# The gate matrix in DRAM by groups of four expert rows

## The chip, the cores and the metric

The kernel runs on one core of one Trainium2 chip. The metric is the device time in microseconds (us) of one execution. Five engines work beside each other: TensorE (PE, with its weight loads PEld), VectorE (DVE), ScalarE (ACT), GpSimd (POOL) and SyncE (SP). Each takes its instructions in a fixed order. Sixteen DMA engines move data between DRAM and the on-chip memory. In this trace q1 is the queue of the transfers that SyncE issues, q10 that of ScalarE's, and q0 that of GpSimd's.

## What is computed

The reference is a block of two layers over 256 latent and 256 context tokens of width 1024. Each layer has a mixer and then PEER, a feed-forward part that chooses among 16384 experts. Only PEER matters here:

```
s      = query . keys                      # 8 heads, 2 halves of 128 keys
idx    = the 16 best pairs (i1, i2) of each head, expert = 128 * i1 + i2
gate   = softmax(their scores)
act    = gelu(x . expert_u[idx])
out    = sum of gate * act * expert_v[idx]
```

Each token so uses 128 of the 16384 experts.

## The kernel before, in words

**Dense over all experts.** For most tokens the kernel doesn't gather: it multiplies every token with every expert and uses a gate that is zero for experts that were not chosen. The experts lie as 128 rows (i1, called `e` in the code) of 128 (i2). For each `e`, `U(e)` multiplies the tokens with the 128 `expert_u` rows of that `e` and applies gelu; `V(e)` multiplies the result with the gates, elementwise, and then with the 128 `expert_v` rows, and adds to the output that stays in PSUM. The experts lie on the partitions, the tokens on the free axis. Layer 0 does so for 384 tokens (three blocks of 128), layer 1 for 192 (a block and a half). The tokens left over (128 in layer 0, 64 in layer 1) are done by gathering rows with GpSimd (`gather_rows`, L1289), their sums on VectorE.

**The gate matrix.** Its entry for i2 = partition p, i1 = e and token t is the gate of expert (e, p) for t, or zero. `gates` (L1195) builds it with one-hot matrices: VectorE compares the chosen indices with a ramp, TensorE multiplies the one-hots of i2 and of i1 for each token, and ScalarE copies the result from PSUM into a tile `gst` of `[128, 128, 32]` (p, e, t) for a group of 32 tokens. There are 12 groups in layer 0 and 6 in layer 1. A full tile (2 MB) is sent to DRAM from ScalarE's queue (L1263), and its first few rows (`HOLD`, 4 in layer 0, 8 in layer 1) are copied to `gt0` on chip. `gst` has two buffers, so a tile can be filled again when the write of the group before the last one has landed.

**The order around it.** While the gates are built, the first U's run already (40 in layer 0, 64 in layer 1). Their results don't all fit: 22 in layer 0 and 32 in layer 1 go out to DRAM through the two buffers of `aout`, from ScalarE's queue too (L1403), and come back as `ain` through SyncE's queue (L1408), asked for two V's ahead, in three buffers. After the gates V starts, at first alone, and then U and V alternate. For every fourth `e`, V asks for the gates of four rows and all groups, through SyncE's queue, in which the weight loads `eraw` (L1356, five buffers), the spilled activations and, in layer 0, eight small loads of scores (L1276) stand as well:

```
gt[0] = p2.tile([128, ng, 4, 32], F32, name="gt", bufs=2)
nc.sync.dma_start(gt[0].rearrange("p g a b -> p g (a b)"),
                  gd.rearrange("g p x -> p g x")[:, :, 32 * e:32 * e + 128])
```

The multiply with the gates is L1423, the split of its result for the matmuls L1426 and L1427, the matmuls of V are L1445, those of U L78 in layer 0 and L1376 and L1380 in layer 1. Casts of weights into a high part are L72 (ScalarE), the low parts L73 (VectorE). `side()` puts the gathers between them.

**What sets the order.** The program is written as one stream, and a planner puts each engine's instructions in order by a modelled timeline, in which every instruction and DMA has a duration of the model. Waits are added by the framework: a DMA that reads a DRAM tile waits for the DMAs that wrote it. So a read of `gd` waits for all its writes.

Of the kernel before, what the change touches and what calls it, by code (L numbers as in the profile page):

```python
# [10 lines left out]
F32 = mybir.dt.float32  # L11
# [19 lines left out]
NI1 = 128  # L31
# [19 lines left out]
class Kernel:  # L51
# [1143 lines left out]
    def gates(self, l, blocks, es, ps):  # L1195

        nc = self.nc
        groups = [(b, tg) for b in blocks for tg in range(2 if b == self.half[l] else 4)]
        gd = self.dp.tile([len(groups), 128, NI1 * 32], F32, name=f"gd{l}", bufs=1)
        sels = {}  # L1200
        with self.pool(f"selx{l}", side="right") as sp:
            exps = {b: self.pick_exp(b, sp, len(blocks)) for b in blocks}
            for b in blocks:
                w = self.pick(b, sp, exps[b])
                if b == self.half[l]:

                    t = sp.tile([128, 128], F32, name="gixf", bufs=1)
# [15 lines left out]
                g = sp.tile([128, 2, 128], F32, name="gsel", bufs=2)  # L1223
# [9 lines left out]
        with self.pool(f"gate{l}", side="right") as p:  # L1233
            for gi, (b, tg) in enumerate(groups):
                sel = sels[b]
                if True:
                    st = p.tile([128, NI1, 32], F32, name="gst", bufs=2)
                    for q in range(32 // OHT):
                        t = 32 * tg + OHT * q
                        ts = (128, OHT, 64, 2)  # L1240
                        io = self.iota.rearrange("p (a b) -> p a b", b=2)[:, None].to_broadcast(ts)
                        at = lambda z: sel[:, z, t:t + OHT][:, :, None].to_broadcast(ts)
                        one = lambda nm: p.tile([128, OHT, 64, 2], F16, name=nm, bufs=OHB)
                        o2, o2s, oh, ol = one("oh2"), one("oh2s"), one("oh1h"), one("oh1l")
                        nc.vector.tensor_tensor(o2, io, at(1), op=OP.is_equal)
                        e = OSC[q % len(OSC)]
                        if e == "a":
                            nc.scalar.mul(o2s, o2, 2.0 ** -12)
                        else:
                            nc.vector.tensor_scalar(o2s, o2, 2.0 ** -12, None, op0=OP.mult)  # L1250
                        nc.vector.tensor_tensor(ol, io, at(0), op=OP.is_equal)
                        nc.vector.tensor_tensor(oh, ol, at(2), op=OP.mult)
                        nc.vector.tensor_tensor(ol, ol, at(3), op=OP.mult)
                        flat = lambda a, z: a[:, z].rearrange("p a b -> p (a b)")
                        for z0 in range(0, OHT, 4):
                            pb = ps.tile([128, 4, 128], F32, name="gps", tag="gps", bufs=GPS)
                            for z in range(4):
                                nc.tensor.matmul(pb[:, z, :], flat(o2, z0 + z), flat(oh, z0 + z), start=True, stop=False)
                                nc.tensor.matmul(pb[:, z, :], flat(o2s, z0 + z), flat(ol, z0 + z), start=False, stop=True)
                            o = OHT * q + z0  # L1260
                            nc.scalar.mul(st[:, :, o:o + 4], pb.rearrange("p t i -> p i t"), 2.0 ** -14)
                    nc.gpsimd.tensor_copy(self.gt0[:, gi], st[:, 0:HOLD[l], :])
                    nc.scalar.dma_start(gd[gi], st.rearrange("p i t -> p (i t)"))  # L1263
        return gd

    def gather_gen(self, l, b, es):
# [61 lines left out]
    def peer(self, l, dense):  # L1328
        nc, i = self.nc, self.i
# [7 lines left out]
        with ExitStack() as es:  # L1337
            p = es.enter_context(self.pool(f"peer{l}"))
# [8 lines left out]
            with self.pool(f"psg{l}", space=PSUM) as gp:  # L1347
                gd = self.gates(l, dense, es, gp)
# [3 lines left out]
            acts, gt, rows, todo, left, los = {}, {}, {}, [], [], []  # L1352

            def stream(src, nm):
                raw = p.tile([128, 1024], F32, name="eraw", bufs=ERAW)
                nc.sync.dma_start(raw, src)  # L1356
                hi = p.tile([128, 1024], F32R, name=nm + "hi", bufs=2)
                lo = p.tile([128, 1024], F32R, name=nm + "lo", bufs=2)
                self.split(hi, lo, raw)
                return hi, lo  # L1360
# [49 lines left out]
            def V(e):  # L1410
                if e < HOLD[l]:
                    gt[0] = self.gt0[:, :, e - e % 4:e - e % 4 + 4]
                elif e % 4 == 0:
                    gt[0] = p2.tile([128, ng, 4, 32], F32, name="gt", bufs=2)
                    nc.sync.dma_start(gt[0].rearrange("p g a b -> p g (a b)"),
                                      gd.rearrange("g p x -> p g x")[:, :, 32 * e:32 * e + 128])
                late = NI1 - 1 - e
                hi, lo = stream(i["v"][l, e], "u" if late < TOGETHER[l] and late % 2 else "v")
                a = acts.pop(e)
                av = a.rearrange("p (g t) -> p g t", t=32)  # L1420

                with self.after(*los[max(e - 2, 0):max(e - 1, 0)]):
                    nc.vector.tensor_tensor(av, av, gt[0][:, :, e % 4, :], op=OP.mult)  # L1423

                w = p2.tile([128, 2 * nt + nt % 128], F32R, name="whl", bufs=max(3, TOGETHER[l]))
                nc.scalar.copy(w[:, 0:nt], a)  # L1426
                self.v_lo = nc.vector.tensor_tensor(w[:, nt:2 * nt], a, w[:, 0:nt].bitcast(F32), op=OP.subtract)  # L1427
                if half is not None:
                    nc.scalar.copy(w[:, 2 * nt:], a[:, nt - nt % 128:])
                los.append(self.v_lo)  # L1430
                todo.append((e, hi, lo, w))
                if 0 < late < TOGETHER[l]:
                    return

                for b in range(nb) if half is None else (1, 0):
                    for hs in ((0,), (1,)) if late == 0 else ((0, 1),):
                        for e_, hi, lo, w in todo:
                            if 128 * b + 128 > nt:

                                ops = [(w[:, 2 * nt - 64:], r) for r in (hi, lo)]  # L1440
                            else:
                                ops = [(w[:, o:o + 128], r) for o, r in ((128 * b, hi), (128 * b, lo), (nt + 128 * b, hi))]
                            for z, (a_, r) in enumerate(ops):
                                for h in hs:
                                    nc.tensor.matmul(acc[b][h], a_, r[:, 512 * h:512 * h + 512],  # L1445
                                                     start=e_ == 0 and z == 0, stop=e_ == NI1 - 1 and z == len(ops) - 1)
                todo.clear()
# [10 lines left out]
            def pubank(shape, nm):  # L1458
                t = pu_.tile([128, 512], F32, name="pu", bufs=8 - 2 * nb)
                n = math.prod(shape[1:])  # L1460
                return t[:, :n] if len(shape) == 2 else t[:, :n].rearrange("p (a b) -> p a b", b=shape[2])
# [19 lines left out]
            for e in range(NI1):  # L1481
                if e == lead - KEEP:
                    es_b.close()
                    if not last:
                        sw = self.s5_ahead(l + 1, es_b.enter_context(self.pool(f"s5w{l + 1}")), pubank)
                back(e + AHEAD)
                if e + KEEP == NI1:
                    for _ in sw:
                        left.append(e)
                    es_b.close()  # L1490
                    ep = es.enter_context(self.pool(f"peere{l}", side="right"))
                    gr = {ty: self.mod_row(l, 5, ty, ep, 1, pubank, f"gaterow{ty}") for ty in sorted({b // 2 for b in dense})}
                V(e)
                if e >= KEEP - 1:
                    side()
                if e + KEEP >= lead and e + KEEP < NI1:
                    U(e + KEEP)
                    side()
                    if e % 4 == 3:
                        next(mg, None)  # L1500
                    if e % 3 == 2:
                        next(sw, None)
# [7 lines left out]
            if half is not None:  # L1510
# [4 lines left out]
                for h in range(2):  # L1515
                    t = ep.tile([128, 512], F32, name="ft", bufs=2)
                    nc.scalar.copy(t, acc[nb - 1][h])
                    b = pubank([128, 512], "fold")
# [4 lines left out]
            for k, b in enumerate(sorted(out) if half is None else (3, 2)):  # L1523
                ty = b // 2
                x = self.xk[b] = self.row([128, 1024], f"xe{b}")
                nc.sync.dma_start(x, self.xd[b])
                st = ep.tile([128, 2], F32, name="fst", bufs=2) if last else self.xst[:, b]
                for h in range(2):
                    hs = slice(512 * h, 512 * h + 512)
                    t = ep.tile([128, 512], F32, name="et", bufs=3)  # L1530
# [14 lines left out]
                else:  # L1545
                    nc.vector.tensor_tensor(st[:, 0:1], st[:, 0:1], st[:, 1:2], op=OP.add)
                    self.rstd(st[:, 1:2], st[:, 0:1], 1024)
                    if k == 0:
                        fg = ep.tile([128, 1024], F32, name="fg", bufs=1)
                        f = i["final_g"]  # L1550
# [126 lines left out]
```

## Time and profile before

| | us |
|---|---|
| median of 3 runs | 2690.12 (2687.3 to 2694.61) |
| the profiled execution | 2692.46 |
| its span, from the first instruction to the last | 2689.2 |
| PE busy | 2525.4 |
| DVE busy | 2185.1 |
| ACT busy | 1217.7 |

The mean granted TensorE clock is 0.972 of full speed. The DMA engines move 694.55 MB, at a mean of 258 GB/s. A share of busy time over the whole span mixes stages with different limits, so the stages are read one by one. The gate matrix is built and written from 540 to 700 us in layer 0 and from 2015 to 2110 in layer 1; V and U with its reads follow, to about 1600 and 2650. In the rows below a line number is that of the kernel before, and "x" a count. PE's busy time is that of pipelined matmuls, whose ends are modelled. The DMA share is the time that packets took, over 16 engines and the stretch; packets that run past the end of a stretch or wait within their time can lift it over 100%.

### The profile page before, as it was taken

What the parts mean: (1) busy time and instruction counts of PE and PEld (TensorE: products, weight loads), DVE (VectorE), ACT (ScalarE), POOL (GpSimd) and SP (SyncE); (2) the same over time, 40 slices, a digit from 0 to 9 for tenths busy, and PEclk for the clock granted to TensorE, in tenths of its full rate; (3) what the DMA queues carried; (4) which work ended last, traced back from release to release, by engine and by line L of the source; (5) the groups of instructions that cost most, each with busy time, mean ns of one, the idle gap of its engine ahead of it and who ended that gap; (6) DMA issues with size and microseconds to landing.
All of it is one profiled execution on the core that took longest, in us unless ns stands there. A gap on an engine that the chain in (4) does not pass through costs nothing.

```text
span 2689.2 us, 42483 instructions
## 1 busy us (share of the span) xinstructions
PE 2525.4 (94%) x15591; PEld 2141.6 (80%) x15591; DVE 2185.1 (81%) x4639; ACT 1217.7 (45%) x2054; POOL 593.8 (22%) x468
## 2 busy tenths in 40 slices
PE   7999999999999999999999999999888977999997
PEld 4776888888778898998899996878877855677786
DVE  8765489999888988998988855837989788999985
ACT  3343343566434333333333333444457644555564
POOL 0001000010004433444443400010001043444500
PEclk8998999999999999999999999989899999999999
DMA  7521432587779899999999956625477899999984
GB/s 271 135 94 41 156 109 93 179 296 280 261 242 371 302 342 333 340 342 331 329 340 335 337 184 176 227 96 192 160 247 264 286 338 331 384 381 381 384 299 141
DMA packets 269200, 694.55 MB, mean 258 GB/s; under 512 B 28608, under 2 KB 120576, under 8 KB 266432
## 3 DMA queue, kind: packets, MB, share of 16 engines
q1 hardware_dynamic: 192960, 430.57, 47.3%
q0 software_dynamic: 55296, 201.35, 20.6%
q10 hardware_dynamic: 20736, 59.92, 6.3%
q8 instruction: 122, 2.00, 0.3%
q14 instruction: 86, 0.70, 0.1%
HBM read 631.84 MB, written 58.56 MB: 257 GB/s over the span
## 4 chain that ended last, share of the span: by engine, by line
PE 41%; issue 12%; DVE 10%; DMA 6%; ACT 4%; ACTq 0%; POOL 0%; SPq 0%; DVEq 0%; POOLq 0%
PE acc L1445 20%; PE pu L78 14%; PE pu L1376 2%; DMA act<-aout 2%; DVE ulo L73 2%; DVE vlo L73 2%; PE pu L1380 1%; ACT uhi L72 1%; DVE grow L1306 1%; DMA ain<-act 1%; ACT vhi L72 1%; PE prT L286 1%; DVE wlo L73 1%; DMA raw<-in_w_in_dram 1%; DVE gacc L1313 1%
## 5 line engine op out<-in xcount | busy, mean ns | idle before, releaser
L1445 PE MATMUL acc<-vhi,whl 128*128 128x512 f32 x2274 | 662.3, 401 | 27.1 <-ACT whl L1426 19.6
L1445 PEld LDWEIGHTS acc<-vhi,whl 128*128 128x128 f32 x2274 | 428.1, 190 | 131.3 <-ACT whl L1426 26.7
L72 ACT CAST vhi<-eraw 128x1024 fp32r<-128x1024 f32 x253 | 265.0, 1048 | 344.1 <-PE acc L1445 308.1
L1445 PE MATMUL acc<-vlo,whl 128*128 128x512 f32 x1264 | 395.4, 404 | 14.5 <-DVE vlo L73 14.0
L78 PE MATMUL pu<-hTb,uhi 128*128 128x384 f32 x2048 | 390.9, 341 | 7.7 <-ACT uhi L72 3.8
L73 DVE TENSOR_TENSOR vlo<-eraw,vhi 128x1024 fp32r<-128x1024 f32 x253 | 309.0, 1223 | 106.9 <-ACT vhi L72 106.3
L1300 POOL DMA_INDIRECT grow<-in_un_dram,gidx x192 | 243.9, 1270 | 603.3 <-DVE grow L1306 198.6
L78 PEld LDWEIGHTS pu<-hTb,uhi 128*128 128x128 f32 x2048 | 362.2, 190 | 17.3 <-ACT actr L1396 4.7
L73 DVE TENSOR_TENSOR ulo<-eraw,uhi 128x1024 fp32r<-128x1024 f32 x259 | 316.7, 1223 | 72.3 <-ACT uhi L72 57.9
L72 ACT CAST uhi<-eraw 128x1024 fp32r<-128x1024 f32 x259 | 272.0, 1051 | 183.5 <-PE pu L78 171.8
L1300 POOL DMA_INDIRECT grow<-in_v_dram,gidx x192 | 271.2, 1412 | 347.1 <-DVE gacc L1313 215.9
L1376 PE MATMUL pu<-hTb,uhi 128*128 128x384 f32 x1024 | 320.7, 369 | 18.0 <-ACT uhi L72 16.0
L1445 PEld LDWEIGHTS acc<-vlo,whl 128*128 128x128 f32 x1264 | 238.9, 191 | 82.8 <-DVE vlo L73 28.7
L1380 PE MATMUL pu<-hTb,ulo 128*128 128x192 f32 x1024 | 250.2, 265 | 25.7 <-DVE ulo L73 24.8
L1313 DVE SCALAR_TENSOR_TENSOR gacc<-grow,gact,gacc 128x1024 f32<-128x1024 f32 x190 | 243.9, 1284 | 1.8 <-DMA grow<-in_v_dram,gidx 1.7
L286 PE MATMUL prT<-hTb,whi 128*128 128x512 f32 (+1 forms) x928 | 240.2, 346 | 3.5 <-ACT whi L72 3.2
L1306 DVE SCALAR_TENSOR_TENSOR grow<-grow,h2n 128x1024 f32<-128x1024 f32 x192 | 234.4, 1221 | 8.8 <-DMA grow<-in_un_dram,gidx 8.8
L1380 PEld LDWEIGHTS pu<-hTb,ulo 128*128 128x128 f32 x1024 | 198.6, 196 | 48.5 <-DVE ulo L73 41.4
L1376 PEld LDWEIGHTS pu<-hTb,uhi 128*128 128x128 f32 x1024 | 195.1, 193 | 27.6 <-ACT uhi L72 22.6
L78 PE MATMUL pu<-hTb,ulo 128*128 128x384 f32 x1024 | 204.0, 337 | 0.5 <-DVE ulo L73 0.5
L73 DVE TENSOR_TENSOR wlo<-raw,whi 128x1024 fp32r<-128x1024 f32 x84 | 102.4, 1220 | 114.0 <-ACT whi L72 111.3
L286 PEld LDWEIGHTS prT<-hTb,whi 128*128 128x128 f32 x928 | 159.8, 190 | 31.3 <-ACT whi L72 3.4
(435 smaller groups left out, 3839.6 us busy)
## 6 DMA issues: line engine op xcount, KB each, us to landing
eraw<-in_ut_dram SPq DMA_DIRECT2D x256, 512.0 KB, 5.6
eraw<-in_v_dram SPq DMA_DIRECT2D x256, 512.0 KB, 6.0
gd<-gst ACTq DMA_DIRECT2D x18, 2048.0 KB, 8.2
mraw<-in_w_mod_dram SPq DMA_DIRECT2D x64, 512.0 KB, 5.1
gt<-gd SPq DMA_DIRECT2D x31, 768.0 KB, 10.2
raw<-in_w_in_dram SPq DMA_DIRECT2D x36, 512.0 KB, 5.3
raw<-in_w_query_dram SPq DMA_DIRECT2D x32, 512.0 KB, 3.9
eraw<-in_w_mod_dram SPq DMA_DIRECT2D x32, 512.0 KB, 6.3
```

Of the source, the lines that this page charges most:

```text
L72: (hi_eng or nc.scalar.copy)(hi, src)
L73: self.last_lo = (lo_eng or nc.vector).tensor_tensor(lo, src, hi.bitcast(F32), op=OP.subtract)
L78: self.nc.tensor.matmul(out, a, b, start=n == 0, stop=n == len(ops) - 1)
L286: self.nc.tensor.matmul(bs[g][:, pt * n:pt * n + n], a[:, k, gs], b, start=z == 0 and k == 0 and q == 0, stop=z == 1 and k == 3 and q == 2)
L1300: nc.gpsimd.indirect_dma_start(out=r, out_offset=None, in_=src, in_offset=bass.IndirectOffsetOnAxis(ap=idx[:, j:j + 1], axis=0))
L1306: v.scalar_tensor_tensor(r, r, 1.0, self.h2n, op0=OP.mult, op1=OP.mult, accum_out=act[:, j:j + 1])
L1313: v.scalar_tensor_tensor(acc, r, act[:, j:j + 1], acc, op0=OP.mult, op1=OP.add)
L1376: both = lambda: nc.tensor.matmul(pu, hi[:, cs], self.hTb[:, :, c, c0:c0 + nt], start=c == 0, stop=c == 7)
L1380: nc.tensor.matmul(pu[:, 0], lo[:, cs], hs(hh, c), start=False, stop=False)
L1445: nc.tensor.matmul(acc[b][h], a_, r[:, 512 * h:512 * h + 512], start=e_ == 0 and z == 0, stop=e_ == NI1 - 1 and z == len(ops) - 1)
```

## The change

The DRAM tile `gd` had the layout (group, partition, e and t): one group of a partition is a piece of 16 KB. After the change it is (e / 4, partition, group, four e's and 32 tokens). A read of four e's is then one piece a partition, of 6 KB in layer 0 (12 groups) and 3 KB in layer 1 (6 groups), where it was 12 or 6 pieces of 512 B. A write of one group is 32 pieces of 512 B a partition, where it was one of 16 KB. Within a partition these pieces lie 768 KB apart in layer 0 and 384 KB in layer 1; the pieces of neighbouring partitions lie 6 KB or 3 KB apart. The tiles on chip, the number of transfers and of bytes, and the queues are the same.

```diff
--- before.py
+++ after.py
@@ -1196,7 +1196,7 @@
 
         nc = self.nc
         groups = [(b, tg) for b in blocks for tg in range(2 if b == self.half[l] else 4)]
-        gd = self.dp.tile([len(groups), 128, NI1 * 32], F32, name=f"gd{l}", bufs=1)
+        gd = self.dp.tile([NI1 // 4, 128, len(groups), 128], F32, name=f"gd{l}", bufs=1)
         sels = {}
         with self.pool(f"selx{l}", side="right") as sp:
             exps = {b: self.pick_exp(b, sp, len(blocks)) for b in blocks}
@@ -1260,7 +1260,8 @@
                             o = OHT * q + z0
                             nc.scalar.mul(st[:, :, o:o + 4], pb.rearrange("p t i -> p i t"), 2.0 ** -14)
                     nc.gpsimd.tensor_copy(self.gt0[:, gi], st[:, 0:HOLD[l], :])
-                    nc.scalar.dma_start(gd[gi], st.rearrange("p i t -> p (i t)"))
+                    nc.scalar.dma_start(gd[:, :, gi, :].rearrange("e p x -> p e x"),
+                                        st.rearrange("p (e i) t -> p e (i t)", i=4))
         return gd
 
     def gather_gen(self, l, b, es):
@@ -1412,8 +1413,7 @@
                     gt[0] = self.gt0[:, :, e - e % 4:e - e % 4 + 4]
                 elif e % 4 == 0:
                     gt[0] = p2.tile([128, ng, 4, 32], F32, name="gt", bufs=2)
-                    nc.sync.dma_start(gt[0].rearrange("p g a b -> p g (a b)"),
-                                      gd.rearrange("g p x -> p g x")[:, :, 32 * e:32 * e + 128])
+                    nc.sync.dma_start(gt[0].rearrange("p g a b -> p (g a b)"), gd[e // 4].rearrange("p g x -> p (g x)"))
                 late = NI1 - 1 - e
                 hi, lo = stream(i["v"][l, e], "u" if late < TOGETHER[l] and late % 2 else "v")
                 a = acts.pop(e)
```

## Rows read from the trace of the kernel before

**Rows 1.** Stages: busy us (count) of PE PEld DVE ACT POOL; clock, DMA share, GB/s.

```profile
540.00:700.00 160.00, 159.64 (x1370) 141.60 (x1373) 142.58 (x222) 104.47 (x162) 12.97 (x12) 1.00 0.82 294
840.00:1600.00 760.00, 760.00 (x3858) 680.82 (x3857) 645.59 (x983) 284.36 (x377) 304.37 (x243) 1.00 0.92 327
2015.00:2105.00 90.00, 77.77 (x699) 71.19 (x697) 86.10 (x139) 67.34 (x125) 13.29 (x5) 0.98 0.75 264
2160.00:2280.00 120.00, 93.15 (x335) 64.38 (x334) 96.71 (x156) 49.25 (x101) 46.68 (x33) 0.94 0.96 342
2290.00:2580.00 290.00, 269.39 (x1373) 222.71 (x1372) 278.54 (x411) 165.08 (x333) 132.45 (x84) 0.99 1.01 381
```

**Rows 2.** Chain of waits in 1480 to 1500: start us, us, what.

```profile
1480.88 4.19 PE pu L78 x24
1485.07 4.21 PE acc L1445 x18
```

**Rows 3.** Waits of VectorE, 2290 to 2580: us in total, times, longest.

```profile
DVE ulo L73 <- ACT uhi L72: 4.6, 12, 0.6
```

**Rows 4.** DMA issues on the page: count, KB each, median us to landing.

```profile
gd<-gst ACTq DMA_DIRECT2D x18, 2048.0 KB, 8.2
...
gt<-gd SPq DMA_DIRECT2D x31, 768.0 KB, 10.2
```

**Rows 5.** DMA queues, 757.1 to 759.3: packets, MB, share of 16 engines.

```profile
q1 hardware_dynamic: 1177, 0.60, 96.1%
```

**Rows 6.** DMA queues, 2077.7 to 2082.2, within one gate write.

```profile
q10 hardware_dynamic: 122, 2.00, 113.5%
q1 hardware_dynamic: 2, 0.00, 0.0%
```

**Rows 7.** DMA queues, 2031.0 to 2034.6, just behind a gate write.

```profile
q10 hardware_dynamic: 304, 0.20, 21.6%
```

**Rows 8.** DMA queues, 2058.5 to 2059.2, a spilled activation alone.

```profile
q10 hardware_dynamic: 144, 0.10, 43.7%
```

**Rows 9.** DMA queues, 939.3 to 943.7, a gate read beside row gathers.

```profile
q1 hardware_dynamic: 1306, 0.67, 53.8%
```

**Rows 10.** DMA queues, 540 to 700.

```profile
q1 hardware_dynamic: 5472, 19.93, 38.9%
```

**Rows 11.** Timeline of ScalarE, 609.3 to 623: two gate writes issued.

```profile
609.54 0.33 ACTq L1263 DMA_DIRECT2D gd<-gst  x1
...
622.65 0.33 ACTq L1263 DMA_DIRECT2D gd<-gst  x1
```

**Rows 12.** Chain of waits, 2010 to 2120, its DMAs.

```profile
2041.22 3.26 DMA act<-aout
...
2045.12 8.94 DMA act<-aout
...
2107.82 8.84 DMA gd<-gst
```

**Rows 13.** Waits of ScalarE, then of VectorE, 2015 to 2105.

```profile
ACT aout L1398 <- DMA act<-aout: 14.6, 6, 3.9
...
DVE aout L1399 <- ACT aout L1398: 3.9, 4, 1.8
```

**Rows 14.** Timelines of SyncE, VectorE and TensorE, 703 to 717.

```profile
704.37 0.43 SPq L1415 DMA_DIRECT2D gt<-gd  x1
...
711.34 1.03 DVE L1423 TENSOR_TENSOR actr<-actr,gt 128x384 f32<-128x384 f32 x2
...
715.18 1.04 PE L1445 MATMUL acc<-vlo,whl 128*128 128x512 f32 x2 [2.49 <-DVE vlo L73]
```

**Rows 15.** Chain of waits, 2160 to 2290, by line.

```profile
by line: PE acc L1445 23.7%; DMA ain<-act 19.6%; issue 18.2%; DVE vlo L73 12.1%; ACT vhi L72 8.9%; DVE grow L1306 8.6%; DVE whl L1427 4.3%; DVE ain L1423 1.8%; ACT whl L1426 1.1%; DVE gacc L1313 1.1%; DVE act L1423 0.9%; ACT whl L1429 0.5%;
```

**Rows 16.** The same chain's longest load, and SyncE's timeline ahead of one.

```profile
2185.05 9.47 DMA ain<-act
...
2182.20 0.38 SPq L1415 DMA_DIRECT2D gt<-gd  x1
```

## The prediction, made before the changed kernel was run

> **What bounds the kernel now.** I read the stage table first, then the chain of waits, then the waits of single engines, then the DMA queues. The stage table cuts the two PEER layers into the parts that the gate matrix passes through [rows 1]. In layer 0 the gate matrix is built and written between 540 and 700 us: TensorE is busy for 159.6 of 160 us. Its long stage, where the matrix is read back (840 to 1600 us), has TensorE busy for all of 760 us, and the chain of waits is nothing but its matmuls back to back, 4.2 us for a U and 4.2 us for a V [rows 2]. In layer 1 it is another engine: while the matrix is written (2015 to 2105) VectorE is busy for 86.1 of 90 us and TensorE for 77.8; in the U-and-V stage (2290 to 2580) VectorE is busy for 278.5 of 290 us, and what it waits for is the ScalarE cast before it [rows 3], not a DMA. Only between 2160 and 2280 is no engine full (PE 93, DVE 97 of 120 us) with the DMA engines at 0.96. So the DMA share of 0.92 to 1.01 in the reading stages looks like a limit and mostly is none: the loads keep up there.
>
> **The change, part by part.** The bytes stay. The instructions stay too: 18 writes from ScalarE's queue, 61 reads from SyncE's, 31 of 768 KB in layer 0 and 30 of 384 KB in layer 1 [rows 4]. What changes is the length of the pieces.
>
> Reads. A read of layer 0 takes 1536 pieces of 512 B, 96 a DMA engine; it becomes 128 pieces of 6 KB, 8 an engine. In a stretch that holds nothing else, 1177 packets of 512 B filled 96.1% of 16 engines for 2.2 us, so one takes 28.7 ns and a read 2.76 us of engine time [rows 5]. For a long piece I go by the 16 KB packets of today's write: 122 in 4.5 us at 113.5% (they run past the end of the stretch) is 670 ns each, or 42 ns a KB [rows 6]; 6 KB is 250 ns, a read 2.0 us. The saving is 0.75 us in layer 0 and half of it, 0.38, in layer 1. Over 31 and 30 reads that is 23 and 11 us of DMA time. In 840 to 1600 and in 2290 to 2580 it buys nothing, because TensorE or VectorE is full there; if that cover were gone it would buy 2 to 3% of the stage, as the share of these packets in it.
>
> Writes. A write is 8 packets of 16 KB on each engine now, 8 x 670 ns = 5.4 us. It becomes 256 packets of 512 B an engine. No row shows a 512 B packet into DRAM. From below it is the 512 B read, 28.7 ns, 7.4 us a write. From above I take a whole 768 B packet of a spilled activation that follows a gate write: 21.6% of 16 engines for 3.6 us, and 0.20 MB are some 256 such packets, so 49 ns, so 12.5 us a write [rows 7]; the same packet in a quiet stretch takes at most 38 ns [rows 8]. I take 28.7: the quiet 768 B packet, longer by half, costs only a third more, so writes are priced as reads are. That adds 2.0 us of DMA time to each of 18 writes, 36 us in all.
>
> More matters how long a write lasts. While today's 16 KB packets run, the other hardware queue gets nothing (q1 at 0.0%) [rows 6]; where the 512 B pieces of a read meet the 4 KB pieces of the row gathers, they get 53.8% of the engines and the gathers nearly all the rest [rows 9]. So the new write will share. SyncE's queue holds 38.9% of the engines while layer 0 writes [rows 10]; I use the same for layer 1. A write of 7.4 us lasts 7.4 us if that queue happens to be idle and 7.4 / 0.61 = 12.1 us beside its mean load. With 1.3 us for the start and the receipt (today: 5.4 us of packets and some 1.5 us of other queues' against a landing of 8.2 us in the median [rows 4]) it lands after 8.7 to 13.4 us; I take 11.5, 3 us later than now.
>
> Who waits for a landing? Four places.
> (a) Layer 0's buffers. The tile that a write empties is filled again by the group after next, in the closest case when the next write is issued, 13.1 us after its own issue [rows 11]. 11.5 fits; 13.4 would cost 0.3 us in a few of ten groups. I take 0, and up to 5 with spilled activations that queue behind.
> (b) Layer 1's spilled activations. They are small writes on the same ScalarE queue, and `aout` has two buffers, so ScalarE waits for one to land before it copies the next. One issued just behind a gate write lands after 8.9 us, one in between after 3.3 [rows 12]. Four gate writes of six have such a write behind them. Each lands 3 us later: 12 us more on top of ScalarE's 14.6. Behind the waiting copy stand the cast of the next U, the evacuation of the gate's PSUM banks and the scaling of the one-hots. VectorE, which bounds here, lost 3.9 us for ScalarE's 14.6 [rows 13], a quarter; by that the price is 3 us, and 12 if nothing hides it. I take 6.
> (c) The last write of layer 0. The first reads wait for all writes on SyncE's queue, ahead of two score loads and the next V loads; the read issued at 704.37 lands about when the multiply by it starts, at 711.34, and TensorE then stands idle for 2.5 us and runs its next matmuls slower [rows 14]. 3 us later, less 0.75 us for the faster read: 2.5 us, on an engine that is full ever after.
> (d) The last write of layer 1 lies on the chain with its whole 8.84 us [rows 12], and a VectorE instruction waits for its buffer. 3 us more.
>
> The only gain is between 2160 and 2280. There the chain passes through loads of spilled activations for 19.6% of 130 us, 25 us [rows 15]; one of them, issued 2.9 us behind a gate read, took 9.5 us [rows 16]. The spilled activations are those of experts 8 to 39, so eight gate reads fall among their loads. Saving only their engine time gives 8 x 0.38 = 3 us; if every second one shortened the load behind it by 2.5 us it would be 10. I take 4.
>
> Sum: 0 + 6 + 2.5 + 3 - 4 = +7.5 us. The profiled execution took 2692.5 us (its span 2689.2 and 3.3 around it), which becomes 2700; it lies 2.4 us above the median of the runs, 2690.1, so I forecast 2697.5.
>
> [...] The new write puts a partition's 32 pieces 768 KB apart (384 KB in layer 1). Today's read does the like without harm: its pieces lie 2 MB apart and cost the 28.7 ns above. [...]
>
> **The rivals.**
> Reads win (faster). What decides is whether a gate read really holds up the activation loads queued behind it in 2160 to 2280. If so it is the 10 us there, and VectorE hides (b) but for 1 us and the five weight buffers hide (c) and (d): 2690 - 9 = 2681. For it: 25 us of that chain are such loads, with the engines at 0.96. Against: only the one shown stands right behind a gate read.
> Scattered writes are dear (much slower). At 49 ns, layer 0's queues would want 0.389 x 160 + 12 x 12.5 = 212 us in a 160 us stage: 50 us more, and about 20 in layer 1 by (b), (c) and (d) with landings near 20 us; 2760. For it: the 49 ns. Against: the 38 ns in quiet.
> The planner moves. The order on every engine comes from a modelled timeline in which these DMAs have a price; another price may put a topk head, a load or a spill elsewhere. The rows show what one place costs: 2.5 us of idle PE at the start of V. Three or four such places are +-10 us: 2688 to 2708 around the forecast.
>
> **How the numbers follow.** Forecast 0.45 (own range 2690 to 2706), reads win 0.20, dear writes 0.10, planner 0.25. A measurement of this kernel tells about 0.3%, 8 us, from no change: faster is below 2682, slower above 2698. Faster: half of reads-win, a third of planner, a little of the forecast, 0.21. Slower: all of dear writes, and two fifths of the forecast and of the planner's case with it, 0.39. The rest is 0.40. For 8 in 10 I go from 2680 to 2720: the bottom takes in reads-win, the top leaves out the dear writes.
>
> **What would show it.** The page's packets under 2 KB fall by some 70,000 for the reads and rise by 73,728 for the writes. A gate write's packets at 27 to 30 ns, its landing at 11 to 12 us; ScalarE's wait for spilled activations in layer 1 at 25 us or more; the first gate reads issued 3 us later after the last write in both layers; gate reads landing in 5 to 7 us; 840 to 1600 and 2290 to 2580 as long as before. The prediction is wrong if landings stay near 8 us (then no loss), if they pass 16 us, or if either long stage changes its length.

## The result: 1.6% slower, outside the range

The changed kernel takes 2733.6 us in the median of its runs (2726.9 to 2736.5), against 2688.9 for the kernel before beside it (2687.3 to 2694.6): a ratio of 1.0165, 95% interval 1.0142 to 1.0188, some 44 us. The forecast was 2697.5 with a range up to 2720. The profiled execution of after took 2732.6 us, its span is 2730.5; that is 41.3 us over the span of before, with the mean granted TensorE clock at 0.965 instead of 0.972.

In after the file has one line more at the gate write and one less at the gate read, so the lines from there to the gate read (now L1416) stand one later than in the rows of before (the issue of a spilled activation was L1403 and is L1404), and those behind it where they were. Every engine runs the same instructions in the same order as before.

The page's DMA part of after shows the pieces as they were counted ahead: ScalarE's queue (q10) has 92160 packets instead of 20736.

```profile
DMA packets 277776, 694.55 MB, mean 254 GB/s; under 512 B 28608, under 2 KB 123648, under 8 KB 277312
...
q10 hardware_dynamic: 92160, 59.92, 7.5%
```

The stage table of after, with the columns and stretches of [rows 1]:

```profile
540.00:700.00 160.00, 151.80 (x1269) 134.68 (x1268) 137.29 (x217) 96.19 (x152) 13.22 (x10) 0.96 0.86 262
840.00:1600.00 760.00, 760.00 (x3843) 678.54 (x3843) 657.69 (x1004) 283.94 (x377) 316.85 (x251) 1.00 0.92 336
2015.00:2105.00 90.00, 69.65 (x540) 63.34 (x539) 72.27 (x119) 53.01 (x95) 14.47 (x7) 0.89 0.72 224
```

While layer 0 writes the gate matrix, TensorE had 159.6 busy us of 160 and now has 151.8; while layer 1 writes, VectorE had 86.1 of 90 and now has 72.3, and the clock is 0.89. (Layer 1's first write comes 21 us later in after; from 2036 to 2126, the same part of its stage, VectorE has 70.5 us and the clock is 0.85.) Layer 0's long stage is as full as ever. So the time went where the matrix is written, and something there stops the engines that were full. ScalarE's timeline names it. In after (start us, us, what; in brackets the idle time ahead and what ended it):

```profile
604.33 0.38 ACTq L1263 DMA_DIRECT2D gd<-gst  x1
604.66 1.07 ACT L1248 ACTIVATE oh2s<-oh 128x1024 f16<-128x1024 f16 x1
605.61 0.50 ACT L1397 ACTIVATE aout<-pu 128x384 f32<-128x384 f32 x1
606.14 7.14 ACTq L1404 DMA_DIRECT2D act<-aout  x1
613.33 1.57 ACT L1261 ACTIVATE gst<-gps 128x512 f32<-128x512 f32 x3 [7.22 <-issue]
```

The same five instructions in before:

```profile
596.23 0.33 ACTq L1263 DMA_DIRECT2D gd<-gst  x1
...
598.04 0.33 ACTq L1403 DMA_DIRECT2D act<-aout  x1
598.43 1.57 ACT L1261 ACTIVATE gst<-gps 128x512 f32<-128x512 f32 x3 [0.42 <-PE gps L1259]
```

The issue of the gate write costs ScalarE 0.38 us, as ever. It is the next issue on the same queue, a spilled activation, that takes 7.14 us instead of 0.33, and ScalarE does nothing until it is through. I call this a hold. After has twelve of more than 1 us: eight in layer 0 (30.1 us together) and four in layer 1 (21.8 us); before has none there. In layer 0 TensorE waits for the evacuation behind it. TensorE's waits, 540 to 700, in after (us in total, times, longest):

```profile
PE gps L1258 <- ACT gst L1261: 8.1, 3, 6.6
```

and in before:

```profile
PE gps L1258 <- ACT gst L1261: 0.2, 1, 0.2
```

In layer 1 the holds are on the chain that ends last. The chain of after, 2040 to 2180; that of before had landings of spilled activations in their place and, at the end, 8.84 us for the last gate write [rows 12]:

```profile
2047.05 4.79 ACTq L1404
...
2069.03 6.14 ACTq L1404
...
2090.39 5.71 ACTq L1404
...
2146.69 13.82 DMA gd<-gst
```

The table below compares seven profiled executions by issue times of gate writes and gate reads (the kernels are those of the experiments). V's end is the last of the matmuls that fold V's output, some 1.9 us behind the last one of L1445.

```
us                            before after  cut    16 x  8 x   spills on GpSimd
                                            writes 1 KB  2 KB  after  before
L0, first to last write       157.8  170.3  169.4  160.7 158.3 157.4  156.4
L0, last write to first read    7.6   14.5   14.3    9.4   8.8  14.6    9.6
from there to L1's first write 1320.4 1317.3 1316.9 1323.7 1320.1 1312.9 1317.3
L1, first to last write        83.1  100.5  104.4   95.7  89.4  85.4   84.2
L1, last write to first read    8.9   13.9   13.9   13.3  13.2  14.1    9.3
L1, first read to V's end     558.9  556.3  556.5  553.1 553.6 556.3  556.5
spill issues over 1 us, L0/L1   0/0  30.1/  31.7/   3.2/ 1.2/0   0/0    0/0
  (sum)                              21.8   23.2   10.0
```

Of the 41.3 us, 36.1 arise in these rows (12.5 + 6.9 - 3.1 + 17.4 + 5.0 - 2.6). The other 5.2 were there before the first gate write, where no instruction differs; the kernel with cut writes (E2) had 3.5 there and those with 16 and 8 pieces -2.1 and 0, so I count them as spread of single executions.

### The profile page after: what moved, and what is told of

Its sections match the earlier page's. It is cut to its first block, busy times and chain, and to the rows that moved or that the text cites. A ratio compares the mean times of both kernels' runs of the same rounds, so it can differ in the third digit from the quotient of the medians.

```text
span 2730.5 us, 42483 instructions
## 1 busy us (share of the span) xinstructions
PE 2537.4 (93%) x15591; PEld 2154.5 (79%) x15591; DVE 2186.4 (80%) x4639; ACT 1216.7 (45%) x2054; POOL 599.1 (22%) x468
## 3 DMA queue, kind: packets, MB, share of 16 engines
q10 hardware_dynamic: 92160, 59.92, 7.5%
## 4 chain that ended last, share of the span: by engine, by line
PE 45%; DVE 10%; issue 9%; ACT 4%; DMA 3%; ACTq 1%; POOL 0%; DVEq 0%; POOLq 0%; SPq 0%
PE acc L1445 22%; PE pu L78 13%; PE pu L1377 3%; PE prT L286 2%; DVE vlo L73 2%; DVE ulo L73 2%; PE pu L1381 2%; ACT uhi L72 1%; DVE grow L1307 1%; ACT vhi L72 1%; ACTq L1404 1%; DVE wlo L73 1%; DMA ain<-act 1%; DVE gacc L1314 1%; PE prN L300 1%
## 5 line engine op out<-in xcount | busy, mean ns | idle before, releaser
L1445 PE MATMUL acc<-vhi,whl 128*128 128x512 f32 x2274 | 660.9, 400 | 25.6 <-ACT whl L1426 18.8
L1445 PEld LDWEIGHTS acc<-vhi,whl 128*128 128x128 f32 x2274 | 427.3, 190 | 129.7 <-ACT whl L1426 25.5
L1445 PE MATMUL acc<-vlo,whl 128*128 128x512 f32 x1264 | 393.9, 402 | 17.3 <-DVE vlo L73 16.6
L78 PE MATMUL pu<-hTb,uhi 128*128 128x384 f32 x2048 | 396.9, 344 | 7.7 <-ACT uhi L72 3.8
L1301 POOL DMA_INDIRECT grow<-in_un_dram,gidx x192 | 248.1, 1292 | 609.3 <-DVE grow L1307 205.0
L78 PEld LDWEIGHTS pu<-hTb,uhi 128*128 128x128 f32 x2048 | 367.6, 192 | 17.4 <-ACT actr L1397 4.7
L1377 PE MATMUL pu<-hTb,uhi 128*128 128x384 f32 x1024 | 326.5, 373 | 28.1 <-ACT uhi L72 27.0
L1445 PEld LDWEIGHTS acc<-vlo,whl 128*128 128x128 f32 x1264 | 237.7, 190 | 85.2 <-DVE vlo L73 31.1
L1377 PEld LDWEIGHTS pu<-hTb,uhi 128*128 128x128 f32 x1024 | 198.4, 196 | 38.1 <-ACT uhi L72 34.0
```

What stands on the lines that cost most here:

```text
L78: self.nc.tensor.matmul(out, a, b, start=n == 0, stop=n == len(ops) - 1)
L1301: nc.gpsimd.indirect_dma_start(out=r, out_offset=None, in_=src, in_offset=bass.IndirectOffsetOnAxis(ap=idx[:, j:j + 1], axis=0))
L1377: both = lambda: nc.tensor.matmul(pu, hi[:, cs], self.hTb[:, :, c, c0:c0 + nt], start=c == 0, stop=c == 7)
```

## Experiments

Theory A: a queue takes only so many pieces that are not yet started; a write of 4096 is over that, and the engine's next issue on that queue is held until the rest fits. Counting in the trace how many of the write's 4096 packets had not started when the held issue ended gives 700 to 1500 in layer 0 and 1280 to 1620 in layer 1. Theory B: a share of each write must have started, about two thirds. Theory C: only the late landing counts, as the forecast had it. Theory D: the engine time of the short packets.

The edits below are shortened: arguments that don't matter are left out, mostly marked by "...". The ratios are to the kernel before, with their 95% intervals.

**E1, long reads alone**, in the kernel before (ratio 0.9989, 0.9973 to 1.0005; 2683.4 us):

```
-gd = tile([len(groups), 128, NI1 * 32])
+gd = tile([128, len(groups), NI1 * 32])   # write gd[:, gi], 16 KB a partition
+nc.sync.dma_start(gt[0]..., gd.rearrange("p g x -> p (g x)")[:, ng * 32 * e:ng * 32 * e + ng * 128])
```

> The write of before (128 pieces of 16 KB) with the reads of the change (one piece of 6 KB, in layer 1 3 KB, per partition): a read takes words that the write left elsewhere, so the gates reach the multiply in another order and the output differs. Every theory that puts the loss into the write expects 2684 us (2680 to 2689): the gate stages as before, the V part of layer 1 some 4 us shorter as in the changed kernel, the rest equal. A theory that blames the longer reads expects over 2700.

No hold, no loss. The small gain can't be put down to the long pieces: its first read in layer 1 was issued 5.9 us after the last write instead of 8.9, since the words it takes come from an early group and not from all of them.

**E2, cut writes alone**, in the changed kernel (1.0150, 1.0113 to 1.0187; 2729.9 us):

```
-gd = tile([NI1 // 4, 128, len(groups), 128])
+gd = tile([NI1 // 4, len(groups), 128, 128])   # write 32 x 512 B, read 12 (6) x 512 B
```

> The write of the change (32 pieces of 512 B per partition, 4096 in all) with the reads of before (12 or 6 pieces of 512 B). Every theory that puts the loss into the write expects 2737 us (2732 to 2742): the whole loss of 44 us, and the 4 us of layer 1's V part not gained. Issues on ScalarE's queue behind a gate write again take 2.4 to 7.1 us. If the reads had a share in the loss it falls short of 2725.

The loss is the write's, though the time lies 2 us under the range given. It holds the same twelve issues, 1.8 to 7.3 us. And the V part that I expected to lose its gain did not: 556.5 us from layer 1's first read to V's end, where the changed kernel with its long reads has 556.3.

**E3 and E5, fewer and longer pieces in the write**, in the changed kernel with reads as before (16 pieces of 1 KB: 1.0069, 1.0044 to 1.0093; 8 of 2 KB: 1.0050, 1.0028 to 1.0073):

```
-gd = tile([NI1 // 4, 128, len(groups), 128])     # write "p (e i) t", i=4
+gd = tile([NI1 // 8, 128, len(groups), 256])     # E3: i=8
+gd = tile([NI1 // 16, 128, len(groups), 512])    # E5: i=16
```

> The write in 16 pieces of 1 KB per partition, 2048 in all, with reads as before. Theory A (a limit on the pieces that are issued and not yet started, some 1000 to 1600 by the changed kernel's trace: the next issue on the queue is held until the rest fits): the next issue is held 0.5 to 2.5 us in place of 2.4 to 7.1, most of the loss goes: 2697 us (2692 to 2705). Theory B (a limit in proportion: about two thirds of a write's pieces must have started): holds of 2.5 to 5 us, about half the loss: 2712 (2705 to 2722). Theory C (no hold matters, the late landing does): by the landing, 10 to 11.5 us with as many pieces at 30 ns more, hardly better than 32 pieces: 2720 to 2735.

> The write in 8 pieces of 2 KB per partition, 1024 in all; reads as before. After the 16-piece run (held until 1117 to 1565 of 2048 pieces were left, 13 us in six holds) theory A puts the limit near 1100 to 1500 pieces, so a write of 1024 should hold nothing: every issue on ScalarE's queue behind a gate write within 0.6 us, and the time of before, 2689 us (2683 to 2695). If the limit goes with the share of the write (theory B), holds of 1 to 3 us stay in layer 1, where the issue follows within 0.8 us, and 2697 (2693 to 2703) remain.

Both run in the order of after. In E3, ScalarE's timeline shows the issue that follows within 0.4 us of the write still held:

```profile
2090.04 0.38 ACTq L1263 DMA_DIRECT2D gd<-gst  x1
2090.45 3.94 ACTq L1404 DMA_DIRECT2D act<-aout  x1
```

while another, 3.3 us behind the write of 610.28, is through at once:

```profile
613.61 0.33 ACTq L1404 DMA_DIRECT2D act<-aout  x1
```

The holds of E3 end with 1117 to 1565 of 2048 pieces not started: 24 to 45% had started, not two thirds. B falls by this share, not by the time: 2707.0 us lies above A's range and in B's. One fixed count, as A has it, doesn't fit either: at 613.61 some 1420 pieces had not started and the issue went through, at 595.9 another was held until 1117 were left. In E5, the issue right behind a write takes 0.74 us:

```profile
2064.51 0.38 ACTq L1263 DMA_DIRECT2D gd<-gst  x1
2064.56 0.38 ACT L1401 ACTIVATE aout<-aout 128x192 f32<-128x192 f32 x1
2064.98 0.74 ACTq L1404 DMA_DIRECT2D act<-aout  x1
```

The one hold left in E5 is 1.22 us (at 598.0), and it begins with some 870 pieces not started. So what holds an issue goes with the number of pieces, but no single number decides: over all these runs ScalarE's holds end with 650 to 1640 pieces not started. Nor is it the bytes: in before an issue goes through in 0.33 us (at 2045.1) with 116 pieces of 16 KB, 1.9 MB, not started, while E3's holds last until 1.1 to 1.6 MB are left. What exactly is counted stays open. E5's median is 2699.5 us, above A's range (to 2695) and in B's: nearly without holds, 13 us remain, of which the table has 6.3 in layer 1's writing stage. There ScalarE waits for spilled activations that land behind the gate write on its queue, 2015 to 2150 (14.6 us in before [rows 13]):

```profile
ACT aout L1399 <- DMA act<-aout: 18.7, 7, 3.9
```

**E4 and E6, no spilled activation behind a gate write**, in the changed kernel (1.0031, 1.0014 to 1.0047; 2695.7 us) and in the kernel before (1.0004, 0.9988 to 1.0020; 2687.4 us):

```
-nc.scalar.dma_start(away[e], acts.pop(e))
+nc.gpsimd.dma_start(away[e], acts.pop(e))
```

> The changed kernel with the spilled activations issued from GpSimd's queue, so that no small issue stands behind a gate write on ScalarE's. The planner places some work of the gate stages otherwise for it. Theory A or B (ScalarE itself is held by its next issue): ScalarE shows no issue over 1 us in the two gate stages; 12 us in layer 0 and some 20 in layer 1 come back: 2700 us (2693 to 2712). Theory C (late landings of the write: buffers, first reads): the landings are as long as in the changed kernel and the time stays at 2728 to 2738. Theory D (DMA engine time of the short packets): the time stays too, 2730.

> Control for the run with the spilled activations on GpSimd's queue: the kernel before with the same move, and the same order of instructions as that run on every engine. Theory A: no issue is held in the kernel before, so the move by itself is worth nothing, 2688 us (2682 to 2694), and the difference of the two, 3 to 12 us, is the price of the short pieces without any hold (later landings). Rival: the move is worth the same in any kernel, and what it gave back to the changed one, 38 us, says nothing of holds: 2650 us.

The decisive pair. Both have one order on every engine (another than that of before and after), and the 4096 pieces are all there in E4; its gate writes end as late as in the changed kernel, their last packets 10 to 17 us after the issue, in layer 1 10.6 to 13.6 against 10.4 to 14.6. C and D expected no change. ScalarE has no issue over 1 us, and layer 0's writing stage is full again in E4:

```profile
540.00:700.00 160.00, 159.26 (x1368) 141.28 (x1370) 142.24 (x222) 104.45 (x162) 29.02 (x27) 1.00 0.94 290
```

The move by itself is worth nothing (E6). E4 takes two things away, the hold and the late landing of a spilled activation behind a write; E5, with the landings and all but one hold gone, tells them apart. Between E4 and E6 lie 0.27%, 7 us (by the two intervals, anything from 1 to 13): that is what the short pieces cost when nothing stands behind them, and in the table it sits in the two steps from a last write to the first read, 5 us each, less 4.4 between the layers.

**E7, the write halved over two queues** (1.0128, 1.0103 to 1.0153; 2721.6 us):

```
+for q, o in ((nc.scalar, 0), (nc.sync, 16)):
+    q.dma_start(gd[o:o + 16, :, gi, :]..., st[:, 4 * o:4 * o + 64]...)
```

> The changed kernel with each gate write halved: the first 16 pieces of a partition from ScalarE's queue, the other 16 from SyncE's, 2048 pieces in each. The planner places some work otherwise. If the limit belongs to the queue that issues (A1), ScalarE's next issues are held as in the 16-piece run, 0 to 2 us in layer 0 and 1.6 to 4 in layer 1, and SyncE's loads behind the other half about as long, which their buffers hide: 2708 us (2698 to 2720). If it belongs to the DMA engines and both queues share it (A2), ScalarE is held 2.4 to 7 us as in the changed kernel: 2732 (2724 to 2745).

Between the two expectations: seven holds, 2.1 to 3.3 us in layer 0 and 3.5 to 4.7 in layer 1, 24.9 us in all. 2048 pieces on ScalarE's queue are held longer than E3's 2048; that the other half, on the same engines at the same time, lets the queue drain more slowly is my reading and was not tried apart. It doesn't decide between A1 and A2; E9 does.

**E9, the gate write from SyncE's queue** (1.0076, 1.0045 to 1.0107; 2707.8 us):

```
-nc.scalar.dma_start(gd[:, :, gi, :]..., st...)
+nc.sync.dma_start(gd[:, :, gi, :]..., st...)
```

> The changed kernel with the gate writes (4096 pieces of 512 B) issued from SyncE's queue, the spilled activations still from ScalarE's. The planner places some work otherwise. Theory A: now SyncE's next load is held behind each write, 2 to 7 us, and no issue of ScalarE lasts over 1 us; a weight load has five buffers, so most of the holds is hidden: 2702 us (2694 to 2716). Rival: holds cost as much on SyncE, because the loads that stand behind are what TensorE and VectorE need: 2730 or more. If ScalarE shows holds all the same, the limit doesn't belong to the queue that issues.

The hold goes with the queue. SyncE's timeline: two loads behind a write take 6.95 us (the first of them 5.67),

```profile
2075.34 0.38 SPq L1263 DMA_DIRECT2D gd<-gst  x1
2075.81 6.95 SPq L1357 DMA_DIRECT2D eraw<-in_ut_dram  x2
```

and ScalarE's, while the first of them is held:

```profile
2079.77 0.33 ACTq L1404 DMA_DIRECT2D act<-aout  x1
```

Nine issues of ScalarE begin while SyncE is held, and each takes 0.33 us. All 18 writes are followed by a hold of SyncE of 2.2 to 6.1 us; its issues over 1 us in the two writing stages come to 92 us (7.5 in before). Yet the stages take 157.9 and 82.6 us, as in before, so the holds are hidden; the five weight buffers are the likely cover. What E9 lost in its profiled execution lies elsewhere: 27 us between the first read of layer 0 and the first write of layer 1. From 1740 to 1780, in layer 1's projections, TensorE ran at 1.2 GHz (granted 0.54 and 0.50), behind a load of a modulation matrix that came 4.7 us late. Part of the planner's other order, I take it; it wasn't tried apart.

```profile
1740.00:1760.00 20.00, 15.94 (x75) 11.30 (x76) 5.95 (x11) 5.55 (x11) 0.00 (x0) 0.54 0.49 164
1760.00:1780.00 20.00, 20.00 (x90) 15.59 (x90) 0.00 (x0) 5.77 (x10) 3.60 (x3) 0.50 0.00 0
```

**E10, the gate write from GpSimd** (1.0055, 1.0037 to 1.0073; 2697.3 us): as E9, with `nc.gpsimd`.

> The changed kernel with the gate writes issued from GpSimd's software queue. In the run with the spilled activations there, an issue of 128 pieces took GpSimd 0.54 us; if that grows with the pieces, 4096 take some 17 us, more than the 13 to 16 us between two gate writes, and each write is late: layer 0 loses 20 us or more, 2715 to 2760. If an issue stays near 0.5 us, theory A expects no hold on ScalarE and the time of the run with the spilled activations on GpSimd, 2696 us (2688 to 2706).

The 17 us were wrong: GpSimd's issue of 4096 pieces takes 1.7 us, and no issue of ScalarE is held. Its time says little of the write: the order on the engines is another, and from layer 1's first read to the end of the span it takes 560.1 us, against 569.9 in after and 572.5 in before. That gain wasn't tried apart.

```profile
593.69 1.69 POOL L1263 DMA_DIRECT2D gd<-gst  x1
```

**E8, a version meant to beat both** (1.0081, 1.0053 to 1.0109; 2710.1 us): layer 0 as before, layer 1 with groups of 16 rows.

```
+gd = tile([NI1 // 16, 128, len(groups), 512]) if l else tile([len(groups), 128, NI1 * 32])
+elif l == 1 and (e % 16 == 0 or e == HOLD[l]):     # 12 KB a partition; the first read half of it
+    gt[0] = tile([128, ng, 16, 32]) ... nc.sync.dma_start(gt[0]..., gd[e // 16]...)
```

> A version meant to beat both: layer 0 as before; in layer 1 groups of 16 expert rows, so that a write is 8 pieces of 2 KB per partition (1024 in all) and a read of 16 rows one piece of 12 KB. Theory A: no issue held, gate stages as before. If the long reads are what shortened layer 1's V part (F), it is 4 to 5 us shorter here too: 2684 us (2678 to 2690). If that gain was only part of the delay given back (G; the kernel with cut writes and short reads showed 3.6 us of it too), 2689.

No hold, but from layer 1's first read to V's end it takes 566.9 us, 13 more than E5 with short reads of 4 rows. A read of 1.5 MB in one go stands ahead of the loads of spilled activations, and half of the 13 us shows as waits for these. VectorE's waits in that part, in E8 (2120 to 2300) and then in E5 (2112 to 2292):

```profile
DVE ain L1438 <- DMA ain<-act: 9.6, 5, 4.0
```

```profile
DVE ain L1423 <- DMA ain<-act: 3.1, 6, 1.3
```

No version here beats the kernel before by more than its measurement can tell.

## Why the prediction was wrong

The step that failed is one that was not there. "Who waits for a landing? Four places" asked only who waits for the write to end, and the issue of the write was left as it was: what it does to the next issue on its queue stands in the sum at nothing, without a row for it. I had the piece count, 4096 in one issue, and asked of it only what a packet costs. The trace of before could have told me the rest, on the other queue. Its writes have 128 pieces, but its reads in layer 0 have 1536, and SyncE's timeline shows what comes behind some of them:

```profile
898.42 0.44 SPq L1415 DMA_DIRECT2D gt<-gd  x1
900.31 5.32 SPq L1454 DMA_DIRECT2D eraw<-in_w_mod_dram  x1
...
1379.44 0.38 SPq L1415 DMA_DIRECT2D gt<-gd  x1
1382.45 2.83 SPq L1356 DMA_DIRECT2D eraw<-in_ut_dram  x1
```

Between 740 and 1600 before has five such issues of 0.99 to 5.32 us, each 1.5 to 3.0 us behind a gate read; after, with 128 pieces a read, has none. (Not every read does it: the loads behind those of 935.6 and 1178.0 go through in 0.33 us with no piece of the read started.) They cost nothing, TensorE being full there, and so I never looked at them; on ScalarE's queue, behind a write of 2.7 times as many pieces, such holds make the result of this change.

The twelve holds on ScalarE, 51.9 us, cost 12.5 us in layer 0's writing stage, all of that stage's loss (E5 and E4 have 0.5 and 1.0 there), and in layer 1 the 17.4 us less the 6.3 that E5 loses without them, 11: together 23.6 of 36.1 us. The other half is covered by ScalarE's slack. In layer 1 TensorE's clock may have a share: granted 0.86 on the mean, between its two levels of 1.2 and 2.4 GHz, from 2046 to 2147 in after, where the engine idles behind ScalarE, and 0.98 in the stage of before [rows 1]; no run prices it. E4 gives back more than 23.6, 36 us by the medians, but it also takes away the landings of (b) and has another order.

Where a rule of the Trainium skill would have spoken, I had not weighed it. By the Trainium skill, "Perfetto Trace Analysis", section "DMA Instruction — HWDGE (DVE, Sync)", the time that the profile gives to an issue begins with a wait for the descriptor generator, which one DMA keeps until all its descriptors are made. The 7.14 us above, behind the write, agree with such a wait. But by the same section of the Trainium skill the write's own issue lasts while its descriptors are made, and it took 0.38 us. The Trainium skill calls the generator shared by two sequencers; E9 has ScalarE through in 0.33 us while SyncE is held, so no sharing shows here.

The steps one by one.
- Packet price 28.7 ns: right. In a stretch of one write, 2069.5 to 2075, against [rows 5 to 7]:

```profile
q10 hardware_dynamic: 2760, 1.41, 92.0%
```

  0.92 x 16 x 5.5 us / 2760 is 29.3 ns; the median is 27. The dear-writes rival (49 ns) is dead: pieces 768 KB apart cost no more than the read's.
- Landing 11.5 us: right as far as it shows. The last packet ends 10.0 to 14.2 us after the issue in layer 0 and 10.4 to 14.6 in layer 1.
- (a), layer 0's buffers, 0: right; ScalarE never waits there for a write to land, only for its own issue.
- (b), layer 1's spilled activations, +6: ScalarE's wait for them was forecast at 25 us or more. In after, 2010 to 2160, it is 10.7, less than the 14.6 of [rows 13]; four holds, 21.8 us, come before it:

```profile
ACT uhi L72 <- issue: 12.1, 2, 6.3
ACT aout L1399 <- DMA act<-aout: 10.7, 5, 4.1
...
ACT act L1401 <- issue: 5.4, 1, 5.4
ACT oh2s L1248 <- issue: 4.9, 1, 4.9
```

  Where no issue of layer 1 is held (E5), the wait is 18.7 and the stage 6.3 us longer: the mechanism was there, smaller than forecast, behind the one that was missed. That a quarter of such waits counts was too low: 4.1 us more of waiting came with 6.3 us more of stage, and the chain of before passes through these landings already [rows 12].
- (c) +2.5 and (d) +3: too small, 6.9 - 3.1 = 3.8 and 5.0 us by the table. The waits are where they were put, on SyncE in both layers (700 to 740, 2140 to 2170):

```profile
SPq L1277 <- DMA gd<-gst: 8.5, 1, 8.5
```

```profile
SPq L1416 <- DMA gd<-gst: 7.9, 1, 7.9
```

- The gain in 2160 to 2280, -4: the time came, the cause was wrong. The stretch to V's end is 2.6 us shorter in after, and 2.4 in E2 with short reads: beside the same write the long reads are worth 0.2 us, and 0.2 again between E4 and E6. What shortened it stays open. Delay given back would fit after, but E1, with long reads and nothing late before them, is 4.0 us shorter, and E3 and E5, with short reads, are 5.8 and 5.3.
- Gate reads landing in 5 to 7 us: their last packets end 7.1 us after the issue in layer 0 and 6.2 in layer 1, in the median.
- Both long stages kept their length, and the planner's order stayed: that rival is out. The reads-win rival is out by E2 beside after.

Without the holds the forecast's terms come to 3.8 + 6.3 + 5.0 - 2.6 = 12.5 us instead of 7.5, where the 6.3 are those of E5 with its longer pieces. The kernels with hardly a hold lie near that: E5 13.4 us over the kernel before by the medians (7.5 to 19.6; 6.7 in its profiled execution), and E4, which has all the short pieces, 8.3 (3.8 to 12.6). So what the forecast did price was about right, in part by luck: (c) and (d) were larger than forecast, (b) hardly showed, and the gain came without the reads. The bulk of the miss is the one mechanism that had no term.

## What to carry to other kernels

Count the pieces of a DMA, not only its bytes: a write of 4096 pieces from a busy engine's hardware queue stops that engine at its next issue, and the profile shows it as a long issue of an innocent small DMA behind it. Keep such a write near or under 1000 pieces (1024 left one hold, of 1.2 us), or issue it from a queue whose engine has time (SyncE's loads with five buffers hid 92 us, GpSimd took 1.7 us a write), or put nothing behind it. Long issues behind many-piece DMAs are in a trace to be found even where they cost nothing yet. And see that the stage that is to gain waits for the reads at all, before writes are cut up to lengthen them.

## What the runs showed of the hardware that was not expected

- Behind a DMA of many pieces, the next issue on the same queue of ScalarE or SyncE was held: 1.2 to 7.3 us instead of 0.33. ScalarE's holds ended with 650 to 1640 pieces of the write not started; the write's own issue took 0.38 us. The other hardware queue went on meanwhile (E9).
- GpSimd's software queue took 128 pieces in 0.54 us and 4096 in 1.7 us, without a hold.
- Write packets into DRAM took 27 ns at 512 B, 46 at 1 KB, 86 at 2 KB and 615 at 16 KB in the median: per KB 54, 46, 43 and 38, so the short pieces of these writes were cheap for the DMA engines. What was dear is their number in one issue.
